# Seven-product FFN: shared sums finished in a PSUM bank, and the products of neighbouring pairs interleaved

## The chip, the cores and the metric

The kernel runs on one core of one Trainium2 chip. The metric is the device time of one execution in microseconds. Before the change, three runs gave 1776.2, 1776.36 and 1777.24 us; the median is 1776.36 us.

A core has TensorE (PE: matrix products, results into PSUM banks), VectorE (DVE), ScalarE (ACT), GpSimd (POOL), and DMA queues that are fed from SyncE (SP) and from GpSimd. Each engine works off its own list of instructions in order and waits on semaphores for the others. PEld in the profile is TensorE's weight load, which overlaps its products.

## The reference

Two layers of an encoder on 512 tokens of width 1024. Each layer has three token mixers (differential attention, a convolution module, neighbourhood attention), merged by gates and an output product, then an FFN and a gated per-layer input. The change is in the FFN:

```python
h = rmsnorm(x, norm_ffn[i])
x = x + (jax.nn.silu(h @ w_ffn_gate[i]) * (h @ w_ffn_up[i])) @ w_ffn_down[i]
```

The FFN is 2816 wide, that is 22 blocks of 128 columns. All is float32.

## The kernel before

Activations are held transposed: features on the 128 partitions, 512 tokens along the free dimension. A float32 product is done as three products of rounded halves: `split` (ScalarE copies the rounded part `hi`, line 143; VectorE subtracts for the rest `lo`, line 157), then hi x hi, hi x lo, lo x hi. So every block of weights is loaded by DMA, split by ScalarE and VectorE, and then used by TensorE.

In the FFN, gate and up product of one block of 128 columns are made together, in `seven` (a "pair"). The two weight blocks side by side and the tokens in two halves of 256 are taken as a 2 x 2 matrix product, which needs seven products of half size in place of eight (Winograd's form). The operands on the token side (b11, b21, b22 and the differences t1 to t4, called `bs`) are made once per layer in `quarters`, at the end of `w_o`. The operands on the weight side are a11, a12 (the gate's two halves), a22 (half of the up block) and the sums s1 to s4; s1 and s2 are summed by GpSimd's adding DMA (line 987) onto loads by SyncE (982, 983), s3 and s4 by VectorE (1003, 1007).

One `product` is four steps of 128 along the contraction, three matmuls of 256 columns each (lines 1017 to 1019): 12 matmuls. A pair has 84. The seven products of a pair run one after the other, in this order: a11b11, a22t4, s2t1, a12b21, s1t3, s3t2, s4b22. Three of them (p1 = a11b11, p4 = a22t4, p5 = s2t1) are needed alone and in a sum; ScalarE copies each to SBUF while its bank goes on collecting. Then VectorE combines: seven operations of 256 columns, which give gg (gate, times the norm's row factor `rb`) and uu (up). The first pair of a layer (`head`) has a different order and two more operations, because `rb` is not there yet. SiLU, the product with uu, and the split into `md` are put off (`pending`) and put out by `flush` in the next pair, behind its copy of p5.

The pairs take their three banks in turn from two groups: the three "mm" banks for an even block, the two "sc" banks and the "av" bank for an odd one. The two "tr" banks serve transposes, in the FFN those of the norm.

The 22 pairs of a layer fall into three parts of 8, 7 and 7 (`PARTS`). After each part the down projection adds its share to x: eight groups of products of 512 columns (`pair` and `gemm`, lines 177 to 179), each read by VectorE.

What sets the order: TensorE's instructions stand in program order. Those of the other engines are put in order by a planner at build time, which works through its own estimate of times and takes, on each engine, the ready instruction with the highest priority; priority is the place in the program, and what loads and splits weights is moved ahead by 400 instructions (`w_ahead`). A few orders are fixed by hand (`behind`). Split weights live in the rotating buffers `wh` and `wl`, three each; a pair uses two (a11|a12 and s1|s2), and the down projection uses the same. a22 has `kh` and `a`, s3|s4 have `spare`, one for even and one for odd blocks. A buffer's next split can begin when TensorE has used its last content. A counter (`chunk2`) gives a tick after every second product, and the norm's transposes and `rb` hang on ticks.

Of the kernel before, what the change touches and what calls it, by code (L numbers as in the profile page):

```python
# [14 lines left out]
AF = mybir.ActivationFunctionType  # L15
ALU = mybir.AluOpType
# [4 lines left out]
P = 128  # L21
# [40 lines left out]
class Net:  # L62
# [109 lines left out]
            self.low = self.split(hi[:, :n], lo[:, :n], raw[:, :n])  # L172
        return hi, lo

    def mm3(self, out, wh, wl, ah, al, first, last):
        mm = self.nc.tensor.matmul
        mm(out, wh, ah, start=first, stop=False)  # L177
        mm(out, wh, al, start=False, stop=False)  # L178
        mm(out, wl, ah, start=False, stop=last)  # L179

    def gemm(self, out, ap, acts, first=True, last=True):

# [661 lines left out]
    def diff_unit(self, head, qt, st4, k2, st, box, ys):  # L844

        nc, i = self.nc, self.i
        half, t = qt // 2, qt % 2
        box[qt] = self.probs(st4, k2, qt, box["s0"])
        if t == 0:
            return  # L850
        yield 3
        ats = [box[2 * half], box[2 * half + 1]]
        pps = []
        for kp in range(2):
            pt = self.ps("tr", (P, 2, 256))
# [12 lines left out]
        cs = slice((head % 2) * P, (head % 2) * P + P)  # L868
        for kp in range(2):
            for u in range(2):  # L870
                v = st["v", head // 2][kp][:, u].rearrange("p (a b) -> p a b", a=2)
                self.mm3(av[:, half * 256:half * 256 + 256], v[:, 0, cs], v[:, 1, cs],
                         pps[kp][:, 0, u], pps[kp][:, 1, u], kp * 2 + u == 0, kp * 2 + u == 3)
        if half == 0:
            return

        eps = self.sb("sm", [P, 4])
        self.stt(eps, box["s0"], EPS, box["s0"], ALU.mult, ALU.mult)
        o = self.sb("t", [P, 512])
# [61 lines left out]
    def quarters(self, x, h, j):  # L941


        one, two = slice(0, 256), slice(256, 512)
        g = lambda k: self.par(self.i, "ffn", k)
        f = []
        for k in (2 * j, 2 * j + 1):
            v = self.sb("t", [P, 512])
            self.act(v, x[k], AF.Copy, scale=g(k))
            f.append(v)  # L950
        b11, b12, b21, b22 = f[0][:, one], f[0][:, two], f[1][:, one], f[1][:, two]
        u = self.sb("t", [P, 2, 256])
        w = self.sb("t", [P, 2, 256])
        t1, t2, t3, t4 = u[:, 0], u[:, 1], w[:, 0], w[:, 1]
        self.tt(t1, b11, b12, ALU.subtract)
        self.tt(t2, b22, t1, ALU.add)
        self.tt(t3, b22, b12, ALU.subtract)
        self.tt(t4, t2, b21, ALU.subtract)
        if j < 2:
            d = [self.sb("rp", [P, 2, 256], F32R) for _ in range(2)]  # L960
            d += [self.sb("b", [P, 2, 256], F32R) for _ in range(2)] if j else \
                self.parts_of("v", [2, 256], 2, F32R)
        else:
            d = [q for n in range(2) for q in self.zs[2 * j - 4 + n]]
        for o, t in zip(d, (t1, t2, t3, t4)):
            self.held = self.split(o[:, 0], o[:, 1], t)
        ha, hb = self.halves(h[2 * j]), self.halves(h[2 * j + 1])
        cut = lambda p, c: (p[0][:, c], p[1][:, c])
        return dict(b11=cut(ha, one), b21=cut(hb, one), b22=cut(hb, two),
                    **{f"t{n + 1}": (o[:, 0], o[:, 1]) for n, o in enumerate(d)})  # L970

    def seven(self, wg, wu, bs, tags, spare, md, first, fb):


        nc = self.nc
        with self.tc.high_priority(offset=min(self.w_ahead, self.tc.cur_priority - self.p0)):
            lo, up = slice(0, 512), slice(512, 1024)
            g, a22 = self.sb("wr", [P, 1024]), self.sb("r", [P, 512])
# [24 lines left out]
            i = self.tt(s3, s1, a22, ALU.add)  # L1003
# [2 lines left out]
                self.behind(i, self.held if fb else self.mark)  # L1006
            self.tt(s4, s3, g[:, up], ALU.add)
            halve(*spare, sums[1], ("s3", "s4"))
        A, C, Q = (self.ps(t, (P, 2, 256)) for t in tags)

        def product(out, w, b, first):
            wh, wl = ws[w]
            mm = nc.tensor.matmul
            for k in range(4):
                c = slice(k * P, k * P + P)
                bh, bl = bs[k][b]
                mm(out, wh[:, c], bh, start=first and k == 0, stop=False, skip_group_check=True)  # L1017
                mm(out, wh[:, c], bl, start=False, stop=False, skip_group_check=True)  # L1018
                mm(out, wl[:, c], bh, start=False, stop=k == 3, skip_group_check=True)  # L1019
            self.chunk2()  # L1020

        o = self.sb("t", [P, 2, 256])
        p1, p4 = o[:, 0], o[:, 1]
        p5 = self.sb("a", [P, 256])
        gg, uu = self.sb("t", [P, 2, 256]), self.sb("t", [P, 2, 256])
        head = fb == 0
        product(A[:, 0], "a11", "b11", True)
        self.act(p1, A[:, 0], AF.Copy)
        if head:
            product(Q[:, 1], "a12", "b21", True)  # L1030
            product(C[:, 0], "s4", "b22", True)
        product(Q[:, 0], "a22", "t4", True)
        self.act(p4, Q[:, 0], AF.Copy)
        five = C[:, int(head)]
        product(five, "s2", "t1", True)
        self.flush(self.act(p5, five, AF.Copy))
        if not head:
            product(A[:, 0], "a12", "b21", False)
        product(Q[:, 0], "s1", "t3", False)
        product(A[:, 1], "s3", "t2", True)  # L1040
        if head:
            self.tt(gg[:, 0], Q[:, 1], p1, ALU.add)
            self.tt(gg[:, 1], C[:, 0], p5, ALU.add)
        else:
            product(C[:, 0], "s4", "b22", False)
        rb = self.rb.rearrange("p (a b) -> p a b", a=2)
        self.tt(p5, p4, p5, ALU.subtract)
        self.tt(gg[:, 0], gg[:, 0] if head else A[:, 0], rb[:, 0], ALU.mult)
        self.tt(p1, A[:, 1], p1, ALU.subtract)
        self.tt(uu[:, 0], p1, Q[:, 0], ALU.subtract)  # L1050
        self.tt(uu[:, 1], uu[:, 0], p5, ALU.add)
        self.tt(gg[:, 1], gg[:, 1] if head else C[:, 0], p1, ALU.subtract)
        self.tt(gg[:, 1], gg[:, 1], rb[:, 1], ALU.mult)

        def rest(then):
            i = self.act(gg, gg, AF.Silu, table="silu")
# [3 lines left out]
            self.held = self.split(*self.halves(md), gg.rearrange("p a b -> p (a b)"))  # L1060

        self.pending.append(rest)

    def behind(self, i, then):

# [17 lines left out]
    def ffn(self, h, x):  # L1083
# [6 lines left out]
        md8.append(tuple(self.sb("e", [P, 512], F32R) for _ in range(2)))  # L1090
        self.sums, self.sevens = [t for _ in range(2) for t in self.parts_of("qk", [1024], 2)], 0
        for part in PARTS:
            mids = []
            for f, fb in enumerate(part):
                tags = (("mm", "mm", "mm"), ("sc", "sc", "av"))[fb % 2]
                md = md8[f]
                mids.append(md)
                wg, wu = self.a["w_fg"][i, fb], self.a["w_fu"][i, fb]
                self.seven(wg, wu, bs, tags, spare[fb % 2], md, part[0] and f < 2, fb)
            self.flush()  # L1100
            down = [self.a["w_fd"][i, m][:, part[0] * P:(part[-1] + 1) * P] for m in range(KD)]
            two = [self.ps(("mm", "sc")[fb % 2 == 0]) for _ in range(2)]
            self.pair(two, down[:2], mids)
            for m in range(KD):
                if m < 2:
                    ps = two[m]
                else:
                    ps = self.ps("mm")
                    self.gemm(ps, down[m], mids)
                d = self.sb("t", [P, 512])  # L1110
                self.tt(d, ps, self.rb, ALU.mult)
                self.tt(x[m], x[m], d, ALU.add)
                if part is PARTS[-1]:
                    if m in (0, 2):
# [352 lines left out]
```

## Time and profile before

| What | Value |
|---|---|
| Median of three runs | 1776.36 us |
| The profiled execution, its span | 1776.7 us |
| TensorE busy | 1767.5 us (99%) |
| TensorE's weight loads busy | 1559.6 us (88%) |
| VectorE busy | 1421.7 us (80%) |
| ScalarE busy | 894.4 us (50%) |
| GpSimd busy | 103.0 us (6%) |
| Granted TensorE clock | digit 9 (90% or more) in every slice |

The profile is one execution, recorded by the hardware. An instruction's row has its start (us from the span's beginning), its duration, engine, line of the kernel, operation, and "out<-in" by the names of the tiles; a name begins with the stage that made it (`ffn_`, `wo_`, `pin_`). In brackets stands the idle time of the engine before it and what ended that. A group's row of waits has total, count and longest. Matmuls overlap in TensorE's pipeline, so the distance from start to start is what one costs, not its duration.

### The profile page before, as it was taken

How to read it: one execution, taken by the hardware profiler on the slowest of the kernel's cores; microseconds unless marked ns; L12 is line 12 of the kernel's file. 1: busy time of each engine (PE TensorE's matmuls, PEld its weight loads, DVE VectorE, ACT ScalarE, POOL GpSimd, SP SyncE). 2: the span in 40 equal slices, each digit the busy share in tenths (PEclk: the TensorE clock that was granted, in tenths of full speed). 3: DMA queues.
4: the chain of work that ended last, by engine and by line, in shares of the span. 5: the costliest groups of instructions: out<-in, count | busy, mean ns of one | idle time of the engine just before them, and what ended most of it. 6: DMA issues, size and time to landing. Idle time of an engine off the chain costs nothing.

```text
span 1776.7 us, 27451 instructions
## 1 busy us (share of the span) xinstructions
PE 1767.5 (99%) x10210; PEld 1559.6 (88%) x10210; DVE 1421.7 (80%) x2418; ACT 894.4 (50%) x1561; POOL 103.0 (6%) x146
## 2 busy tenths in 40 slices
PE   9999999999999999999999999999999999999998
PEld 7888888888899899998888888888888998989987
DVE  7878887998798587787776788889887976867776
ACT  5577555225565254454545765452356643534454
POOL 0000000000111010100000000000001110101000
PEclk9999999999999999999999999999999999999999
DMA  5666641334757366543447655423357664655332
GB/s 202 188 186 176 161 125 42 113 98 140 230 150 193 109 167 160 132 131 123 145 124 198 176 165 149 113 71 95 93 179 198 171 179 115 173 144 151 98 108 92
DMA packets 113509, 256.07 MB, mean 144 GB/s; under 512 B 14560, under 2 KB 19424, under 8 KB 113376
## 3 DMA queue, kind: packets, MB, share of 16 engines
q1 hardware_dynamic: 99984, 229.93, 42.3%
q0 software_dynamic: 12672, 23.07, 8.3%
q8 instruction: 81, 1.33, 0.3%
q10 hardware_dynamic: 720, 1.31, 0.2%
q14 instruction: 52, 0.43, 0.1%
HBM read 215.46 MB, written 7.34 MB: 125 GB/s over the span
## 4 chain that ended last, share of the span: by engine, by line
PE 96%; DVE 2%; ACT 1%; issue 0%; DMA 0%; POOL 0%; ACTq 0%; POOLq 0%; DVEq 0%
PE ffn_mm L1017 4%; PE ffn_mm L1019 4%; PE ffn_mm L177 4%; PE ffn_mm L179 4%; PE ffn_mm L178 4%; PE ffn_mm L1018 4%; PE ffn_sc L1019 3%; PE ffn_sc L1017 3%; PE ffn_sc L1018 3%; PE mergea_mm L177 2%; PE mergea_mm L178 2%; PE mergea_mm L179 2%; PE diff_sc L811 2%; PE gatec_mm L177 2%; PE gatec_mm L178 2%; PE gatec_mm L179 2%
## 5 line engine op out<-in xcount | busy, mean ns | idle before, releaser
L160 DVE SCALAR_TENSOR_TENSOR conv_z<-glu_z,pre_par,conv_z 128x512 f32<-128x512 f32 x240 | 179.4, 748 | 3.3
L143 ACT ACTIVATE ffn_wh<-ffn_wr 128x1024 fp32r<-128x1024 f32 (+1 forms) x92 | 92.7, 1014 | 111.7 <-PE ffn_mm L178 77.1
L987 POOL DMA_DIRECT2D ffn_qk<-w_fu x88 | 78.0, 990 | 605.7 <-DMA ffn_qk<-w_fu 414.7
L157 DVE TENSOR_TENSOR ffn_wl<-ffn_wr,ffn_wh 128x1024 fp32r<-128x1024 f32 (+1 forms) x92 | 107.4, 1173 | 5.4 <-ACT ffn_wh L143 4.9
L157 DVE TENSOR_TENSOR ffn_t<-ffn_mm,wo_rb 128x512 f32<-128x512 f32 (+1 forms) x64 | 38.6, 604 | 67.9 <-PE ffn_mm L179 67.8
L143 ACT ACTIVATE mergea_wh<-mergea_wr 128x1024 fp32r<-128x1024 f32 (+1 forms) x32 | 27.1, 846 | 96.8 <-PE mergea_mm L178 79.6
L143 ACT ACTIVATE ffn_wh<-ffn_qk 128x1024 fp32r<-128x1024 f32 x44 | 46.7, 1060 | 35.9 <-PE ffn_mm L178 15.7
L157 DVE TENSOR_TENSOR ffn_wl<-ffn_qk,ffn_wh 128x1024 fp32r<-128x1024 f32 x44 | 53.8, 1224 | 11.3 <-ACT ffn_wh L143 11.3
L157 DVE TENSOR_TENSOR ffn_t<-ffn_t,ffn_t 128x512 f32<-128x512 f32 (+1 forms) x46 | 31.3, 680 | 31.4 <-ACT ffn_t L143 30.9
L143 ACT ACTIVATE diff_a<-diff_sc,diff_s 128x512 f32<-128x512 f32 x32 | 22.0, 686 | 61.0 <-DVE diff_s L902 61.0
L177 PE MATMUL ffn_mm<-ffn_v,ffn_wh 128*128 128x512 f32 x132 | 51.4, 389 | 0.0
L178 PE MATMUL ffn_mm<-ffn_v,ffn_wh 128*128 128x512 f32 x132 | 51.4, 389 | 0.0
L179 PE MATMUL ffn_mm<-ffn_v,ffn_wl 128*128 128x512 f32 x132 | 51.3, 389 | 0.0
L177 PE MATMUL ffn_mm<-ffn_y,ffn_wh 128*128 128x512 f32 x132 | 51.3, 389 | 0.0
L178 PE MATMUL ffn_mm<-ffn_y,ffn_wh 128*128 128x512 f32 x132 | 51.3, 389 | 0.0
L179 PE MATMUL ffn_mm<-ffn_y,ffn_wl 128*128 128x512 f32 x132 | 51.3, 389 | 0.0
L1019 PE MATMUL ffn_mm<-wo_h,ffn_wl 128*128 128x256 f32 x176 | 49.8, 283 | 0.0
L1019 PE MATMUL ffn_sc<-wo_h,ffn_wl 128*128 128x256 f32 x176 | 49.8, 283 | 0.0
L1018 PE MATMUL ffn_mm<-wo_h,ffn_wh 128*128 128x256 f32 x176 | 49.8, 283 | 0.0
L1018 PE MATMUL ffn_sc<-wo_h,ffn_wh 128*128 128x256 f32 x176 | 49.8, 283 | 0.0
L1017 PE MATMUL ffn_sc<-wo_h,ffn_wh 128*128 128x256 f32 x176 | 49.8, 283 | 0.0
L1017 PE MATMUL ffn_mm<-wo_h,ffn_wh 128*128 128x256 f32 x176 | 49.8, 283 | 0.0
(876 smaller groups left out, 6588.6 us busy)
## 6 DMA issues: line engine op xcount, KB each, us to landing
ffn_qk<-w_fu POOLq DMA_DIRECT2D x88, 256.0 KB, 5.7
ffn_wr<-w_fg SPq DMA_DIRECT2D x44, 512.0 KB, 3.7
ffn_wr<-w_fd SPq DMA_DIRECT2D x32, 448.0 KB, 3.9
ffn_r<-w_fu SPq DMA_DIRECT2D x44, 256.0 KB, 3.7
ffn_qk<-w_fg SPq DMA_DIRECT2D x44, 256.0 KB, 4.3
ffn_qk<-w_fu SPq DMA_DIRECT2D x44, 256.0 KB, 4.6
natten_wr<-w_in SPq DMA_DIRECT2D x16, 512.0 KB, 4.3
natten_b<-bias SPq DMA_DIRECT2D x32, 256.0 KB, 4.0
```

What stands on the lines that cost most here:

```text
L143: i = self.nc.scalar.activation(out, in_, func, **kw)
L157: return self.nc.vector.tensor_tensor(out, a, b, op)
L160: return self.nc.vector.scalar_tensor_tensor(out, a, s, b, op0, op1)
L177: mm(out, wh, ah, start=first, stop=False)
L178: mm(out, wh, al, start=False, stop=False)
L179: mm(out, wl, ah, start=False, stop=last)
L811: self.nc.tensor.matmul(out, st4[:, u, qs], st[:, ks], start=n == 0, stop=n == 1)
L987: nc.gpsimd.dma_start(q, wu[:, lo], accum_op=ALU.add)
L1017: mm(out, wh[:, c], bh, start=first and k == 0, stop=False, skip_group_check=True)
L1018: mm(out, wh[:, c], bl, start=False, stop=False, skip_group_check=True)
L1019: mm(out, wl[:, c], bh, start=False, stop=k == 3, skip_group_check=True)
```

## The change

The seven products are the same. Three of the combinations now happen in the banks. The bank C gets a11b11; ScalarE copies it into the bank A; s3t2 is added onto it there (t2 and t4 have changed sign in `quarters`); ScalarE copies that sum from A into Q. Then A collects s2t1 and later s4b22, C collects a12b21, and Q collects a22t4. s1t3 goes to a bank of the "tr" group and is copied to `uu`; the sum in A after s2t1 is copied there too. VectorE is left with four operations: two sums for uu and the two products with `rb`. uu comes out with its sign turned, so the down projection's result is subtracted from x.

`seven` becomes a generator in steps, and `sevens_of` runs the steps of two neighbouring pairs in turn: step 1 of the next pair, step 4 of this one, step 2 of the next, step 5 of this one, step 3 of the next. For pairs after the first, this gives the order: next a11b11; this s2t1, a22t4; next s1t3; this s4b22; next s3t2, a12b21. The first pair of a part runs its steps 1 to 3 alone, the last its steps 4 and 5 alone. The first pair of a layer (`early`) has s4b22 in a "tr" bank, as its second product, followed by a12b21.

In the attention's `diff_unit` the two halves of the "av" bank now share one start flag (`mm3` passes on the extra argument).

```diff
-    def mm3(self, out, wh, wl, ah, al, first, last):
+    def mm3(self, out, wh, wl, ah, al, first, last, **kw):
...
-                         pps[kp][:, 0, u], pps[kp][:, 1, u], kp * 2 + u == 0, kp * 2 + u == 3)
+                         pps[kp][:, 0, u], pps[kp][:, 1, u], half + kp + u == 0,
+                         half * kp * u == 1, skip_group_check=True)
...
-        self.tt(t2, b22, t1, ALU.add)
+        self.stt(t2, t1, -1.0, b22, ALU.mult, ALU.subtract)
...
-        self.tt(t4, t2, b21, ALU.subtract)
+        self.stt(t4, t2, -1.0, b21, ALU.mult, ALU.subtract)
...
-        A, C, Q = (self.ps(t, (P, 2, 256)) for t in tags)
+        C, A, Q = (self.ps(t, (P, 256)) for t in tags)
...
+        def corner():
+            product(C, "a12", "b21")
+            if not early:
+                self.tt(gg[:, 0], C, self.halved(0), ALU.mult)
+
+        product(C, "a11", "b11", True)
+        self.act(A, C, AF.Copy)
+        yield
+        if early:
+            Z = self.ps("tr", (P, 256))
+            product(Z, "s4", "b22", True)
+            self.act(gg[:, 1], Z, AF.Copy)
+            corner()
+            yield
+        T = self.ps("tr", (P, 256))
+        product(T, "s1", "t3", True)
+        self.act(uu[:, 0], T, AF.Copy)
+        yield
+        product(A, "s3", "t2")
+        self.flush(self.act(Q, A, AF.Copy))
+        if not early:
+            corner()
+        yield
+        product(A, "s2", "t1")
+        self.act(uu[:, 1], A, AF.Copy)
+        product(Q, "a22", "t4")
+        self.tt(uu[:, 1], uu[:, 1], uu[:, 0], ALU.add)
+        self.tt(uu[:, 0], Q, uu[:, 0], ALU.add)
+        if early:
+            self.tt(gg[:, 0], C, self.halved(0), ALU.mult)
+            self.tt(gg[:, 1], A, gg[:, 1], ALU.add)
+        yield
+        if not early:
+            product(A, "s4", "b22")
+        self.tt(gg[:, 1], gg[:, 1] if early else A, self.halved(1), ALU.mult)
...
+    def sevens_of(self, pairs, head):
+        def go(*gens):
+            for g in gens:
+                next(g, None)
+        pairs = iter(pairs)
+        one = next(pairs)
+        go(one, one, one)
+        if head:
+            go(one)
+        for two in pairs:
+            go(two, one, two, one, two)
+            one = two
+        go(one, one)
...
-                self.tt(x[m], x[m], d, ALU.add)
+                self.tt(x[m], x[m], d, ALU.subtract)
```

The removed lines of `seven` are its block of products and the seven operations, which stand in the listing above.

More of the change, by code (lines that the diff above doesn't have):

```diff
@@ L173, in weights @@
         return hi, lo
-    def mm3(self, out, wh, wl, ah, al, first, last):
+    def mm3(self, out, wh, wl, ah, al, first, last, **kw):
         mm = self.nc.tensor.matmul
-        mm(out, wh, ah, start=first, stop=False)
-        mm(out, wh, al, start=False, stop=False)
-        mm(out, wl, ah, start=False, stop=last)
+        mm(out, wh, ah, start=first, stop=False, **kw)
+        mm(out, wh, al, start=False, stop=False, **kw)
+        mm(out, wl, ah, start=False, stop=last, **kw)
     def gemm(self, out, ap, acts, first=True, last=True):
@@ L970, in quarters, with seven @@
                     **{f"t{n + 1}": (o[:, 0], o[:, 1]) for n, o in enumerate(d)})
-    def seven(self, wg, wu, bs, tags, spare, md, first, fb):
+    def seven(self, wg, wu, bs, tags, spare, md, first, fb, early):
         nc = self.nc
@@ L1008, in seven, with product @@
             halve(*spare, sums[1], ("s3", "s4"))
-        A, C, Q = (self.ps(t, (P, 2, 256)) for t in tags)
-        def product(out, w, b, first):
+        C, A, Q = (self.ps(t, (P, 256)) for t in tags)
+        def product(out, w, b, first=False):
             wh, wl = ws[w]
@@ L1020, in product @@
             self.chunk2()
-        o = self.sb("t", [P, 2, 256])
-        p1, p4 = o[:, 0], o[:, 1]
-        p5 = self.sb("a", [P, 256])
         gg, uu = self.sb("t", [P, 2, 256]), self.sb("t", [P, 2, 256])
[L1026 to L1053, printed above, removed]
+        def corner():
+            product(C, "a12", "b21")
+            if not early:
+                self.tt(gg[:, 0], C, self.halved(0), ALU.mult)
@@ L1062, in seven, with halved @@
         self.pending.append(rest)
+    def halved(self, n):
+        return self.rb[:, n * 256:n * 256 + 256]
+    def sevens_of(self, pairs, head):
[11 more added lines that the diff above has]
+        go(one, one)
     def behind(self, i, then):
@@ L1092, in ffn @@
         for part in PARTS:
[L1093 to L1099, printed above, removed]
+            mids = md8[:len(part)]
+            self.sevens_of((self.seven(self.a["w_fg"][i, fb], self.a["w_fu"][i, fb], bs,
+                                       (("mm", "mm", "mm"), ("sc", "sc", "av"))[fb % 2],
+                                       spare[fb % 2], md8[f], part[0] and f < 2, fb, fb == 0)
+                            for f, fb in enumerate(part)), part[0] == 0)
             self.flush()
             down = [self.a["w_fd"][i, m][:, part[0] * P:(part[-1] + 1) * P] for m in range(KD)]
-            two = [self.ps(("mm", "sc")[fb % 2 == 0]) for _ in range(2)]
+            two = [self.ps(("mm", "sc")[part[-1] % 2 == 0]) for _ in range(2)]
             self.pair(two, down[:2], mids)
```

## The prediction

> **What bounds the kernel now.** I read the page's shares and chain first, then TensorE's waits, then the windows of the stage that is changed, then three stretches of its timelines.
>
> ```profile
> span 1776.7 us, 27451 instructions
> ...
> PE 1767.5 (99%) x10210; PEld 1559.6 (88%) x10210; DVE 1421.7 (80%) x2418; ACT 894.4 (50%) x1561; POOL 103.0 (6%) x146
> ...
> PE 96%; DVE 2%; ACT 1%; issue 0%; DMA 0%; POOL 0%; ACTq 0%; POOLq 0%; DVEq 0%
> ```
>
> TensorE is busy for 99% of the span and is 96% of the chain that ended last. Its own waits in the whole program are four:
>
> ```profile
> PE pre_av L325 <- DVE pre_zeror L398: 1.1, 1, 1.1
> PE natten_tr L734 <- ACT natten_e L143: 0.3, 2, 0.2
> PE natten_tr L736 <- ACT natten_e L143: 0.3, 2, 0.2
> PE natten_tr L736 <- DVE natten_a L157: 0.2, 1, 0.2
> ```
>
> None is in the FFN, which is what the change touches. Busy spans of overlapping matmuls can hide small holes, so I count starts too. The window from the first product of layer 0 to the end of the eighth pair:
>
> ```profile
> 495.93:577.09 81.16, 81.16 (x681) 81.16 (x680) 72.92 (x125) 48.95 (x81) 13.51 (x15) 1.00 0.70 179
> ```
>
> The columns are PE, PEld, DVE, ACT, POOL, clock, DMA. Eight pairs are 8 x 7 x 12 = 672 matmuls plus 8 transposes; at one start each 0.12 us the matmuls alone are 80.6 of the 81.16 us. The 0.12 us and the length of a product come from these rows (the first rows of the layer's products):
>
> ```profile
> 495.93 0.28 PE L1017 MATMUL ffn_mm<-wo_h,ffn_wh 128*128 128x256 f32 x1
> ...
> 497.24 0.28 PE L1019 MATMUL ffn_mm<-wo_h,ffn_wl 128*128 128x256 f32 x1
> 497.36 0.28 PE L1017 MATMUL ffn_mm<-wo_h,ffn_wh 128*128 128x256 f32 x1
> ...
> 498.80 0.60 PE L213 MATMUL wo_tr<-pre_ident,wo_ss 128*128 128x128 f32 x4
> 499.15 0.36 PE L1017 MATMUL ffn_mm<-wo_h,ffn_pt 128*128 128x256 f32 x1
> ```
>
> A product takes 497.36 - 495.93 = 1.43 us, a pair 7 x 1.43 = 10.0 us. So the FFN runs at TensorE's issue rate without a hole. What the other engines save there is worth nothing by itself; the change can gain only by a faster matmul, and can lose by any wait it puts before one.
>
> **The change, part by part.** *TensorE.* 84 matmuls of the same width per pair before and after, with the same weights and moving operands in each of the seven products; the down projection is untouched. Cost 0. The tick that issues the norm's two groups of transposes still falls after the second and the sixth product: cost 0.
>
> *VectorE.* The block behind the products shrinks from seven operations of 256 columns to four (gg0, two sums for uu, gg1):
>
> ```profile
> 641.93 0.42 DVE L157 TENSOR_TENSOR ffn_a<-ffn_t,ffn_a 128x256 f32<-128x256 f32 x1
> ...
> 644.05 0.42 DVE L157 TENSOR_TENSOR ffn_t<-ffn_t,wo_rb 128x256 f32<-128x256 f32 x1
> ```
>
> These are the first and the last of the seven. 42 pairs save 3 each, the two first pairs 9 - 5 = 4 each: 134 x 0.42 = 56 us of VectorE's 1421.7. TensorE covers all of it now, so it is worth 0. Subtracting in place of adding into x costs the same. Eight of `quarters`' 32 additions per layer become the three-operand form; One of them on 256 columns can hardly cost more than twice the 0.42, so 0 to 16 x 0.42 = 7 us of VectorE, near 0 by the nearest row, and covered likewise (the last quarter's operands are wanted no earlier than the fourth product, as now).
>
> *ScalarE.* Three copies out of the banks become four (C to A, T to uu, A to Q, A to uu), five in a first pair: 42 + 4 = 46 more. No row shows a copy that writes a bank; the rows below give 0.36 to 0.38 for one that reads it, and wo_z's row further down 0.40 from SBUF to SBUF, so about 0.36 to 0.40, some 17 us in all on an engine that is 50% busy. What counts is when they end, since TensorE now waits for three of them. The steady pair, ScalarE:
>
> ```profile
> 642.35 0.38 ACT L143 ACTIVATE ffn_t<-ffn_mm 128x256 f32<-128x256 f32 x1 [2.05 <-PE ffn_mm L1019]
> 643.66 0.63 ACT L143 ACTIVATE ffn_kh<-ffn_r 128x512 fp32r<-128x512 f32 x1 [0.92 <-PE ffn_mm L1018]
> 644.20 0.36 ACT L143 ACTIVATE ffn_t<-ffn_mm 128x256 f32<-128x256 f32 x1
> 645.21 0.38 ACT L143 ACTIVATE ffn_a<-ffn_mm 128x256 f32<-128x256 f32 x1 [0.65 <-PE ffn_mm L1019]
> 645.49 0.62 ACT L143 ACTIVATE ffn_t<-ffn_t 128x512 f32<-128x512 f32 x1
> 646.58 1.06 ACT L143 ACTIVATE ffn_wh<-ffn_qk 128x1024 fp32r<-128x1024 f32 x1 [0.47 <-ACT ffn_t L143]
> 647.55 0.61 ACT L143 ACTIVATE ffn_v<-ffn_t 128x512 fp32r<-128x512 f32 x1
> 648.07 1.04 ACT L143 ACTIVATE ffn_y<-ffn_qk 128x1024 fp32r<-128x1024 f32 x1
> 649.01 1.04 ACT L143 ACTIVATE ffn_wh<-ffn_wr 128x1024 fp32r<-128x1024 f32 x1
> ```
>
> It idles for 2.05, 0.92 and 0.65 us in front of work that TensorE releases. The new steady order, with "one" the earlier pair and "two" the next, is: two a11b11, one s2t1, one a22t4, two s1t3, one s4b22, two s3t2, two a12b21. Copy A to Q must end before one's s2t1, with two products between (2.87 us); A to uu before s4b22, two products (2.87 us); C to A before s3t2, four products (5.7 us). Today's copies have two, two and three products to spare. A copy of 0.38 behind one split of 1.06 is 1.44 us, half of the room. Cost 0.
>
> *Buffers for weights.* The split pieces (`wh`, `wl`: three buffers, two used per pair) are freed in another order. The piece s1|s2 of the next pair takes the buffer of a11|a12; the row at 646.58 shows it start just when a12's product has ended:
>
> ```profile
> 646.45 0.28 PE L1017 MATMUL ffn_mm<-wo_v,ffn_wh 128*128 128x256 f32 x1
> ...
> 647.68 1.23 DVE L157 TENSOR_TENSOR ffn_wl<-ffn_qk,ffn_wh 128x1024 fp32r<-128x1024 f32 x1 [0.23 <-ACT ffn_wh L143]
> ```
>
> The first row starts the product after a12's. Both halves are done at 648.91, 2.5 us after the release. Now five products (7.2 us) lie between release and use; after the change three (4.3 us): 1.8 us to spare, each pair. For a11|a12 the room goes from nine products to five, for s3|s4 from twelve to seven. Cost 0, but this is the thinnest place of the steady state. The loads themselves (SP's four and POOL's two adding ones per pair) are the same; they are issued three products earlier in the program and still wait for the same raw buffers; the adding load's 5.7 us to landing is far below a 10 us pair with three raw buffers.
>
> ```profile
> ffn_qk<-w_fu POOLq DMA_DIRECT2D x88, 256.0 KB, 5.7
> ```
>
> *The first pair of a layer.* Its order becomes a11b11, s4b22, a12b21, s1t3, s3t2. The third product adds into C, so it waits until C is copied to A, and only one product lies between. ScalarE at this place now:
>
> ```profile
> 497.79 0.40 ACT L143 ACTIVATE wo_z<-wo_t 128x256 fp32r<-128x256 f32 x1
> 498.10 0.58 ACT L143 ACTIVATE pin_t<-pin_sc 128x512 f32<-128x512 f32 x1
> 498.57 0.40 ACT L143 ACTIVATE wo_z<-wo_t 128x256 fp32r<-128x256 f32 x1
> 498.88 1.06 ACT L143 ACTIVATE ffn_wh<-ffn_qk 128x1024 fp32r<-128x1024 f32 x1
> 499.85 0.70 ACT L143 ACTIVATE wo_z<-wo_t 128x256 fp32r<-128x256 f32 x2
> 500.46 0.58 ACT L143 ACTIVATE pin_t<-pin_sc 128x512 f32<-128x512 f32 x1
> 500.94 0.37 ACT L143 ACTIVATE ffn_t<-ffn_mm 128x256 f32<-128x256 f32 x1
> ```
>
> The last row is the copy of the same a11b11 product, which ended at about 497.5: it came 3.4 us late, behind work that is earlier in the program, and nobody minded. The third product is due at 499.15. If the copy stood where it stands now, TensorE would wait until 501.31 + 0.1 (a hand-over as above): 2.2 us. But the 1.06 us split at 498.88 needs the buffer that a12b21 frees (it starts right at that release), so it falls behind the copy: the two wo_z go to 498.88, pin_t to 499.5, the copy to about 500.0, the third product to about 500.45. Wait 1.3 us. If the planner takes the copy in the slot at 498.10, the wait is 0. I take 1.3, by the row it is nearest to, per layer; both ends, 0 and 2.2, stay for the range. Behind this wait stand all later products; what feeds them has then 1.3 us more room.
>
> *The ends of the three parts.* The last pair of a part has no partner, so its A to Q copy has one product of room (1.43 us) and its A to uu copy likewise, with the next down-projection splits in the queue. ScalarE does at such an end now:
>
> ```profile
> 572.92 1.06 ACT L143 ACTIVATE ffn_wh<-ffn_wr 128x1024 fp32r<-128x1024 f32 x1 [0.47 <-ACT ffn_t L143]
> 573.89 0.61 ACT L143 ACTIVATE ffn_y<-ffn_t 128x512 fp32r<-128x512 f32 x1
> 574.41 1.04 ACT L143 ACTIVATE ffn_wh<-ffn_wr 128x1024 fp32r<-128x1024 f32 x1
> ```
>
> The first copy meets an idle engine: 0. For the second, count from the end of a12b21: split 1.0, md half to 1.6, second split (released at 1.4, ahead in priority) to 2.6, copy to 2.95, against 2.87 due: 0.15 us of wait with the hand-over, or 0 if copy and split change places, or 0.35 if the md half ends 0.2 later. I take 0.07 x 6 = 0.4, between the first two. First pairs of parts 2 and 3 need C to A within one product, with one 1.06 us split released 1.43 us before: 0.
>
> Sum: 2 x 1.3 + 0.4 + zeros = +3.0 us. The profiled execution was 1776.7 us, 0.3 above the median of 1776.36; on the median this is 1779.4.
>
> **A page of the Trainium skill against the row.** Three rows of TensorE's timeline, two neighbours in the first pair and the start of a product in a steady one:
>
> ```profile
> 501.62 0.28 PE L1019 MATMUL ffn_mm<-wo_z,ffn_a 128*128 128x256 f32 x1
> 501.73 0.28 PE L1017 MATMUL ffn_mm<-wo_z,ffn_kh 128*128 128x256 f32 x1
> ...
> 642.15 0.28 PE L1017 MATMUL ffn_mm<-wo_v,ffn_kh 128*128 128x256 f32 x1
> ```
>
> The first two are 0.11 us apart, where a product's mean is 1.43 / 12 = 0.12. The Trainium skill ("TensorE: Matmul & The Clock Gate", Back-to-back issue gap) gives N / 2.4 + 2.5 ns, 109 ns for 256 columns, as the warm gap of an isolated stream; by it a pair is 0.9 us shorter than the trace has it, and something would be holding TensorE. The trace does not agree, and the measurement decides.
>
> **The rivals.**
> (1) *Hidden anyway.* ScalarE's planner puts the copy into an early slot, all other room holds: +0, 1776.4. For it: the gaps above; against it: the copy that came 3.4 us late.
> (2) *Slower, by the steady state.* The split of s1|s2 slips past its 1.8 us. It now stands behind the A to Q copy and the SiLU, and the SiLU waits for gg1, whose product ended only one product before. It decides when ScalarE reaches the split more than 1.8 us after the release. 38 pairs have a predecessor in their part; at 0.3 us each +11 us, 1791 with the first pairs; at 0.7, 1806. Against it: copy and SiLU are 0.38 + 0.62 = 1.0 us and start one product, 1.43 us, before the release; VectorE is lighter than now.
> (3) *More at the first pair.* The copy at its present place (2.2 us a layer), A to Q late as well and the ends at their worst (6 x 0.35): 4.4 + 2.1 = 6.5, 1782.9.
> (4) *Faster matmuls.* The 0.12 us is held up by VectorE's or ScalarE's traffic and falls to the 0.11 that some rows have: 44 x 84 x 0.01 = 37 us, 1739. Against it: from 642.15 to the row at 646.45 three products take 1.43 us each while ScalarE idles for a third of the time, the same as at 495.93, where it has no gap.
>
> **How the numbers follow.** The forecast (wait of one to two microseconds in each layer's first pair, little else; 1778.4 to 1781) gets 0.45, hidden 0.22, steady state 0.18, more at the first pair 0.10, faster matmuls 0.05. About what a measurement can tell from no change is 0.2%, 3.55 us, so the line lies at 1779.9. Of the forecast two thirds are under it. Faster: 0.05. Same: 0.30 + 0.22 = 0.52. Slower: 0.15 + 0.18 + 0.10 = 0.43. The range takes in the forecast, hidden, more at the first pair, and the lower third of the steady state: 1775.6 to 1788, leaving out some 0.17; the forecast's own is 1778.4 to 1781.
>
> **What the changed profile would show.** A wait of TensorE at the third product of each layer, for ScalarE's copy, 1 to 1.5 us long, with the copy right behind a pin_t; no other TensorE wait in the FFN over 0.3 us; the window of eight pairs 81 to 83 us long; VectorE's busy time some 56 us lower, ScalarE's 17 higher; 0.12 us between the products' matmuls. The prediction is wrong if waits recur in each pair at s1t3, s2t1 or s4b22, or if the copy is taken at once.

## The result and the profile after

The changed kernel takes 1782.47 us (median of five runs, 1781.2 to 1784.88), the kernel before 1776.36 (1776.2 to 1777.24): the ratio is 1.0034, with a 95% interval from 1.0022 to 1.0045. The change costs some 6 us, about twice the forecast's 3; that is a third of a per cent, small but clear of the noise.

The page of the changed kernel, its span, busy times and chain:

```profile
span 1783.1 us, 27425 instructions
...
PE 1773.3 (99%) x10210; PEld 1561.7 (88%) x10210; DVE 1377.8 (77%) x2284; ACT 917.0 (51%) x1607; POOL 103.4 (6%) x146
...
PE 95%; DVE 3%; ACT 1%; issue 1%; POOL 0%; DMA 0%; ACTq 0%; POOLq 0%; DVEq 0%
```

VectorE has 44 us less to do and ScalarE 23 us more. TensorE does the same 10210 matmuls, is still 99% busy, and gets longer. Its own waits (total, count, longest):

```profile
PE ffn_mm L1020 <- DVE ffn_pt L157: 2.0, 2, 1.0
PE pre_av L325 <- DVE pre_zeror L398: 1.1, 1, 1.1
PE wo_tr L227 <- POOL wo_rc L223: 0.4, 2, 0.2
```

The first and the last are new. Both come once in each layer, and neither is the one that was forecast. The window from the first product of layer 0 to the end of its eighth pair:

```profile
498.73:582.43 83.70, 82.47 (x682) 81.51 (x681) 66.16 (x103) 53.38 (x90) 13.76 (x15) 0.95 0.70 176
```

It was 81.16 us and is 83.70 (the window ends 0.1 us into the down projection). How long a layer's FFN takes on TensorE is read from its first product to the last transposes that bear its name, those of the norm behind it. These rows give the transposes' first and last start, of the kernel before:

```profile
L227 PE MATMUL ffn_tr<-pre_ident,ffn_rc x4: 271/272/273, 848.8 to 849.1; 128*128 128x128 f32 x4
```

and the same group and the first product, of the changed kernel:

```profile
L227 PE MATMUL ffn_tr<-pre_ident,ffn_rc x4: 271/272/278, 854.2 to 854.5; 128*128 128x128 f32 x4
...
498.73 0.28 PE L1018 MATMUL ffn_mm<-wo_h,ffn_wh 128*128 128x256 f32 x1
```

Before: 849.1 - 495.93 = 353.2 us. After: 854.5 - 498.73 = 355.8 us. With hundredths from the starts it is 353.17 and 355.77 in both layers: 2.60 us more per layer, 5.2 in all. That is the change. (This one execution began the first layer's FFN 2.7 us later than the same kernel did when it was profiled once more: 498.73 against 496.04. The span of the second profile is 2.6 us shorter, so these 2.6 us don't belong to the change; the last section comes back to it.)

Where the 2.60 us of a layer lie is seen by comparing each matmul's start with the next one's, 0.12 us apart where nothing waits:

| Place in the layer | Longer than before, us |
|---|---|
| third pair, s3t2 | 0.21 + 0.10 + 1.16 + 0.10 = 1.57 |
| second pair, the norm's last transposes | 0.33 |
| first pair, s1t3 | 0.14 + 0.10 = 0.24 |
| end of part 1, s4b22 | 0.11 + 0.10 = 0.21 |
| ends of parts 2 and 3, s4b22 | 0.08 + 0.08 = 0.16 |
| sum | 2.5 of 2.6 |

The largest is the third pair's s3t2. TensorE there, in the changed kernel:

```profile
523.03 0.28 PE L1020 MATMUL ffn_sc<-wo_h,ffn_y 128*128 128x256 f32 x1
523.36 0.39 PE L1018 MATMUL ffn_mm<-wo_rp,ffn_pt 128*128 128x256 f32 x1
523.59 0.28 PE L1019 MATMUL ffn_mm<-wo_rp,ffn_pt 128*128 128x256 f32 x1
524.87 0.39 PE L1020 MATMUL ffn_mm<-wo_rp,ffn_pt 128*128 128x256 f32 x1 [1.00 <-DVE ffn_pt L157]
```

`ffn_pt` is the buffer of s3|s4 of this pair. VectorE in the same stretch:

```profile
519.19 0.69 DVE L157 TENSOR_TENSOR ffn_v<-ffn_t,ffn_v 128x512 fp32r<-128x512 f32 x1
519.79 0.68 DVE L157 TENSOR_TENSOR ffn_qk<-ffn_qk,ffn_r 128x512 f32<-128x512 f32 x1
520.39 1.22 DVE L157 TENSOR_TENSOR ffn_wl<-ffn_wr,ffn_wh 128x1024 fp32r<-128x1024 f32 x1
521.53 0.68 DVE L157 TENSOR_TENSOR ffn_qk<-ffn_qk,ffn_wr 128x512 f32<-128x512 f32 x1
...
523.60 1.22 DVE L157 TENSOR_TENSOR ffn_pt<-ffn_qk,ffn_pt 128x1024 fp32r<-128x1024 f32 x1
```

The first row is the end of the split of the first pair's result into `md`. The second is the sum s3 of the third pair, right behind it; the fourth is s4; the last is the low half of s3|s4, done at 524.82, where TensorE wanted it with its third matmul at 523.7. The same work in the kernel before:

```profile
516.90 0.68 DVE L157 TENSOR_TENSOR ffn_v<-ffn_t,ffn_v 128x512 fp32r<-128x512 f32 x1
517.50 0.68 DVE L157 TENSOR_TENSOR ffn_qk<-ffn_qk,ffn_r 128x512 f32<-128x512 f32 x1
...
520.25 1.23 DVE L157 TENSOR_TENSOR ffn_pt<-ffn_qk,ffn_pt 128x1024 fp32r<-128x1024 f32 x1
```

Counted from the layer's first product, VectorE begins its half of `md`'s split at 20.97 us before and 20.46 after, and the low half of s3|s4 is done at 25.55 and 26.09: nearly the same. What moved is the use. s3t2 was the twentieth product and is the seventeenth; it starts 28.09 us after the first product before (at 524.02) and 24.63 after. The 2.8 us of room turned into a wait of 1.2. That s3 comes directly behind `md` is no accident of VectorE: `seven` sets an order for s3 by hand in the first three pairs of a layer (`if first or fb < 3: self.behind(i, self.held ...)`), and in the third pair what it stands behind is the split of the first pair's `md`.

The step that the forecast had priced, a12b21 in the first pair, shows no wait. ScalarE at this place:

```profile
500.59 0.36 ACT L143 ACTIVATE ffn_mm<-ffn_mm 128x256 f32<-128x256 f32 x1
500.89 1.42 ACT L143 ACTIVATE wo_z<-wo_t 128x256 fp32r<-128x256 f32 x4
502.22 1.07 ACT L143 ACTIVATE pin_t<-pin_sc 128x512 f32<-128x512 f32 x2
503.17 0.39 ACT L143 ACTIVATE ffn_t<-ffn_tr 128x256 f32<-128x256 f32 x1
```

The first row is the copy from C to A. It is done at 500.95, a microsecond ahead of a12b21 (501.97); the `wo_z` and `pin_t` copies come behind it, not ahead. What is late instead is the last row, the copy of s4b22 out of the "tr" bank: s1t3, due at 503.48, needs that bank and starts at 503.61. And the norm's small sums, VectorE first, then GpSimd:

```profile
502.78 0.69 DVE L216 TENSOR_REDUCE wo_sm<-wo_tr 128x4 f32<-128x512 f32 x1
...
503.72 1.22 DVE L157 TENSOR_TENSOR ffn_wl<-ffn_wr,ffn_wh 128x1024 fp32r<-128x1024 f32 x1
504.85 1.22 DVE L157 TENSOR_TENSOR ffn_wl<-ffn_qk,ffn_wh 128x1024 fp32r<-128x1024 f32 x1
...
506.59 0.17 DVE L219 TENSOR_SCALAR wo_sm<-wo_sm 128x4 f32<-128x4 f32 x1
```

```profile
506.84 1.46 POOL L223 TENSOR_TENSOR wo_rc<-wo_sm,pre_power 128x4 f32<-128x4 f32 x1 [8.89 <-DVE wo_sm L219]
```

Two weight splits got between the reduction and the small sum behind it, so GpSimd ends at 508.30, and the transposes that were due at 508.0 start at 508.35.

### The profile page after: what moved, and what is told of

Read it like the earlier page. It is cut to its first block, busy times and chain, and to the rows that moved or that the text cites. A ratio compares the mean times of both kernels' runs of the same rounds, so it can differ in the third digit from the quotient of the medians.

```text
span 1783.1 us, 27425 instructions
## 1 busy us (share of the span) xinstructions
PE 1773.3 (99%) x10210; PEld 1561.7 (88%) x10210; DVE 1377.8 (77%) x2284; ACT 917.0 (51%) x1607; POOL 103.4 (6%) x146
## 4 chain that ended last, share of the span: by engine, by line
PE 95%; DVE 3%; ACT 1%; issue 1%; POOL 0%; DMA 0%; ACTq 0%; POOLq 0%; DVEq 0%
PE ffn_mm L178 4%; PE ffn_mm L177 4%; PE ffn_mm L179 4%; PE ffn_mm L1020 3%; PE ffn_mm L1018 3%; PE ffn_mm L1019 3%; PE ffn_sc L1018 3%; PE ffn_sc L1020 3%; PE ffn_sc L1019 3%; PE mergea_mm L178 2%; PE mergea_mm L177 2%; PE mergea_mm L179 2%; PE diff_sc L811 2%; PE gatec_mm L177 2%; PE gatec_mm L178 2%; PE gatec_mm L179 2%
## 5 line engine op out<-in xcount | busy, mean ns | idle before, releaser
L157 DVE TENSOR_TENSOR ffn_t<-ffn_mm,wo_rb 128x512 f32<-128x512 f32 (+1 forms) x86 | 47.8, 556 | 71.7 <-PE ffn_mm L179 61.4
L143 ACT ACTIVATE natten_wh<-natten_wr 128x1024 fp32r<-128x1024 f32 x24 | 25.4, 1058 | 41.7 <-issue 15.2
```

Source lines behind the costliest of these rows:

```text
L143: i = self.nc.scalar.activation(out, in_, func, **kw)
L157: return self.nc.vector.tensor_tensor(out, a, b, op)
```

## The experiments

All ratios are against the kernel before on the same chip, whose medians were 1776.8 to 1777.13 us on the three chips used; the column "Against before" is the one to compare. "FFN" is the stretch measured above, one layer.

| Kernel | Median, us | Ratio, 95% interval | Against before, us | FFN, us |
|---|---|---|---|---|
| before | | | | 353.17 |
| the change again | 1782.29 | 1.0032, 1.0019 to 1.0044 | +5.2 | 355.76 |
| shorter hold | 1779.24 | 1.0013, 1.0004 to 1.0022 | +2.1 | 354.25 |
| + norm's sums earlier | 1778.51 | 1.0008, 1.0000 to 1.0017 | +1.4 | 353.86 |
| no interleaving | 1794.29 | 1.0098, 1.0085 to 1.0112 | +17.2 | 361.57 |
| + bank and part ends | 1776.88 | 1.0002, 0.9992 to 1.0011 | +0.1 | 353.23 |
| VectorE's work given back | 1778.82 | 1.0012, 1.0004 to 1.0021 | +2.0 | 354.15 |
| before, hold and flag alone | 1777.02 | 1.0001, 0.9992 to 1.0010 | +0.2 | 353.17 |
| the copy late | 1783.95 | 1.0037, 1.0023 to 1.0051 | +6.9 | 356.76 |

**The change again.** The changed kernel as it is, beside the experiments.

> The changed kernel as it is, on the same chip as its variants. Its profile lost time in two ways: 1.7 us in the opening, where this one execution was granted a clock of 0.949 for the first 36 us, and 5.1 us in the FFN (2.55 per layer). If the opening belongs to that execution alone, this profile has the opening as before and TensorE's waits in the FFN as before: 1.16 us for ffn_pt at the third pair of each layer, 0.34 at wo_tr, 0.24 at the first pair's s1t3. Then the median is 5 to 6 us over the kernel before. If the opening's loss belongs to the change, it is there again.

It measured 1782.29 us (1781.23 to 1783.68), with the same new waits of TensorE, 1.0 us for `ffn_pt` in each layer. The opening is as before: the first FFN product starts at 496.04 us, against 495.93 in the kernel before. So the opening's loss belonged to the one execution. (The expectation has the lower clock in its first 36 us alone; the trace has 0.95 in the FFN's window too.)

**The hold one pair shorter.** The hand-set order no longer covers the third pair.

```diff
-            if first or fb < 3:
+            if first or fb < 2:
                 self.behind(i, self.held if fb else self.mark)
```

> The changed kernel, but the order by hand that puts the third pair's s3 = s1 + a22 behind the split of the first pair's result is dropped (fb < 2 in place of fb < 3). Theory: in the new order that result is split later and s3|s4 is needed earlier, so this order by hand makes TensorE wait 1.16 us (1.6 with the matmuls beside it) at the third pair's s3t2; without it the wait goes, 3 us in two layers. Rival: s3|s4 is late because VectorE's queue is full there (a split of 1.22 us stands between s3 and s4); then dropping the order moves it by less than 0.5 us.

1779.24 us, 3.0 us less than the change. TensorE's waits start like this, with none in the FFN's products:

```profile
PE pre_av L325 <- DVE pre_zeror L398: 1.1, 1, 1.1
PE wo_tr L227 <- POOL wo_rc L223: 0.4, 2, 0.2
```

VectorE makes the third pair's sums and the low half before the first pair's `md`:

```profile
509.94 0.69 DVE L157 TENSOR_TENSOR ffn_qk<-ffn_qk,ffn_r 128x512 f32<-128x512 f32 x1
...
512.69 1.23 DVE L157 TENSOR_TENSOR ffn_pt<-ffn_qk,ffn_pt 128x1024 fp32r<-128x1024 f32 x1
...
517.00 0.69 DVE L157 TENSOR_TENSOR ffn_v<-ffn_t,ffn_v 128x512 fp32r<-128x512 f32 x1
```

s3t2 starts at 519.97 here, 6 us after the low half is done. So the hold was the cause, and VectorE had the time. It accounts for 1.5 of the 2.6 us a layer.

**The norm's small sums earlier as well.** Their priority is raised above that of the weight splits, and so is that of the copy of s4b22 in a layer's first pair.

```diff
-        with self.tc.high_priority(offset=min(200, ...) ...):
+        with self.tc.high_priority(offset=min(600 if self.phase == "wo" else 200, ...) ...):
             sm = self.sb("sm", [P, 4])
...
-            self.act(gg[:, 1], Z, AF.Copy)
+            with self.tc.high_priority(offset=min(400, self.tc.cur_priority - self.p0)):
+                self.act(gg[:, 1], Z, AF.Copy)
```

> The changed kernel without that order, and with two instructions moved ahead in priority: the norm's small sums in front of the first pair's splits (TensorE waited 0.34 us at wo_tr), and the copy of Z ahead of the copies of the input product (TensorE waited 0.24 us for its bank). Theory: the three waits are all that the FFN lost except the end of a part, so the FFN comes within 0.5 us of its time before and the run within 1 us (0.06%) of the kernel before. Rival: something of the change that is not a wait in the FFN costs the rest; then 2 us or more stay.

1778.51 us. The transposes' wait is gone, and the FFN is 0.39 us a layer shorter. It is still 0.7 us a layer above the kernel before and the run 1.4, where the theory had the run within 1 us. The copy did not move, and s1t3's delay (0.15 + 0.10 us) stayed. Priority alone didn't bring that copy forward, and the part ends were not touched here.

**No interleaving.** The changed kernel, with all five steps of one pair ahead of the next pair's.

```diff
-        for two in pairs:
-            go(two, one, two, one, two)
-            one = two
-        go(one, one)
+        for one in pairs:
+            go(one, one, one, one, one, one)
```

(The three lines ahead of the loop, which start the first pair, go too.)

> The changed kernel without the interleaving: each pair runs its seven products in one piece. Theory: then each copy between banks has one product (1.43 us) of room in every pair, as it now has at the ends of parts, where 0.08 to 0.22 us were lost; three such places in 44 pairs give 0.1 to 0.3 us a place, 13 to 40 us slower than the change. Rival: a copy takes 0.4 us and needs no more than 1.43; then it costs under 3 us and the interleaving was worth nothing.

1794.29 us, 12.0 us more than the change, just under the 13 to 40 expected. TensorE's waits in the FFN:

```profile
PE ffn_sc L1018 <- ACT ffn_t L143: 2.6, 2, 1.3
PE ffn_mm L1018 <- ACT ffn_t L143: 1.9, 2, 1.0
...
PE ffn_mm L1018 <- ACT ffn_mm L143: 0.9, 2, 0.5
PE ffn_mm L1020 <- DVE ffn_pt L157: 0.9, 2, 0.4
```

These lie in the first three pairs of a layer. Most of the later pairs add about 0.21 us in front of s4b22, too short for the list of waits: the copy from A to `uu` has one product of room in each pair here, which in the change only the last pair of a part has. So the interleaving pays for itself: the copies through the banks need the second product between them.

**The remaining short rooms.** On top of the shorter hold and the earlier norm: the first pair's bank for s4b22 comes from the "av" group, and in the last pair of a part s1t3 moves behind a22t4.

```diff
-            Z = self.ps("tr", (P, 256))
+            Z = self.ps("av", (P, 256))
...
-        T = self.ps("tr", (P, 256))
-        product(T, "s1", "t3", True)
-        self.act(uu[:, 0], T, AF.Copy)
-        yield
+        def side():
+            T = self.ps("tr", (P, 256))
+            product(T, "s1", "t3", True)
+            self.act(uu[:, 0], T, AF.Copy)
+        if not tail:
+            side()
+            yield
...
         product(Q, "a22", "t4")
+        if tail:
+            side()
```

(The raised priority of the copy of s4b22 is taken back; in the last pair, the flush of the pair before it goes one step further down.)

> The version with the shorter hold, the norm's earlier small sums, and two more edits: the first pair's bank for s4b22 comes from the av group (so s1t3 no longer waits for its copy), and in the last pair of a part s1t3 stands behind a22t4, so that two products lie between each ScalarE copy and its use. Theory (what is left of the loss are these single short rooms): the waits in front of s1t3 (0.25 us a layer) and at the end of part 1 (0.2 us a layer, 0.08 at parts 2 and 3) go, 1 to 1.3 us in all; the FFN's TensorE starts take 683.0 to 683.3 us where the kernel before takes 682.9, and the run is within 0.5 us of the kernel before. Rival (something steady costs TensorE a little in each pair): it stays 1 us or more above the kernel before. Second rival (the moved product only shifts the wait, to the down projection's first splits behind md): no gain over the version before it, 1.4 us above the kernel before.

1776.88 us against 1776.8 for the kernel before. The FFN takes 353.23 us a layer against 353.17; the FFN's matmul starts alone, which the expectation counts over both layers with the work between them left out, add up to 683.0 us against 682.9. The only wait at the head of TensorE's list is an old one outside the FFN:

```profile
PE pre_av L325 <- DVE pre_zeror L398: 1.1, 1, 1.1
```

So the places in the table of the result explain the loss, and nothing steady is left in the pairs. The new order, mended, is as fast as the old one; no version here is faster.

**VectorE's work given back.** The version with the norm's earlier sums, with three additions per pair whose result nothing uses.

```diff
         self.tt(uu[:, 0], Q, uu[:, 0], ALU.add)
+        dump = self.sb("t", [P, 2, 256])
+        for _ in range(3):
+            self.tt(dump[:, 0], uu[:, 0], uu[:, 1], ALU.add)
```

> The version with the shorter hold and the norm's earlier small sums, plus three VectorE additions of 256 columns in each pair, whose results nothing uses: VectorE gets back about what the change took from it (132 x 0.33 to 0.42 = 44 to 55 us). Theory (VectorE's saved time is covered by TensorE and worth nothing): the same time as that version within 0.5 us, 1.4 us above the kernel before, and VectorE's busy time back at 1420 us. Rival (the lighter VectorE is what keeps the new order's waits small): 3 us or more slower than that version, with waits of TensorE for VectorE's subtractions in the FFN.

```profile
PE 1768.6 (100%) x10210; PEld 1559.2 (88%) x10210; DVE 1419.4 (80%) x2416; ACT 910.3 (51%) x1607; POOL 108.0 (6%) x146
```

VectorE is back at 1419.4 us, 42 more than without the additions. The run is 1778.82 us, 2.0 above the kernel before where the version without them is 1.4 above, and the FFN is 0.29 us a layer longer: 0.28 of it in front of the second pair's s4b22. The intervals of the two runs overlap; the rows of the two layers give 0.58 us. So 42 us of VectorE are worth about 0.6 us. That is a little over the 0.5 that I had allowed, and far from the rival's 3.

**Two parts on the old order.** The kernel before, with the shorter hold and the attention's shared start flag.

```diff
-                         pps[kp][:, 0, u], pps[kp][:, 1, u], kp * 2 + u == 0, kp * 2 + u == 3)
+                         pps[kp][:, 0, u], pps[kp][:, 1, u], half + kp + u == 0,
+                         half * kp * u == 1, skip_group_check=True)
...
-            if first or fb < 3:
+            if first or fb < 2:
```

> The kernel before, with two things alone: the shared start flag of the attention's av bank, and the shorter hand-set order (pairs 1 and 2 of a layer in place of 1 to 3). Theory (the hold costs only together with the new order, and the flag costs nothing): 0 within 0.5 us, and no wait of TensorE in the FFN. Rival (the hold is a loss in either order, so that the shorter one is a gain of its own): 2 to 3 us faster than the kernel before, which would make the mended version's gain no property of the change.

1777.02 us against 1776.8, and the same 353.17 us a layer. The hold costs nothing in the old order, and neither does the flag.

**The copy late.** The changed kernel, with the order that the forecast had assumed: in a layer's first pair, the copy from C to A stands behind the token operands' last split.

```diff
-        self.act(A, C, AF.Copy)
+        i = self.act(A, C, AF.Copy); early and self.behind(i, self.held)
```

> The changed kernel, with one order by hand: in a layer's first pair the copy of a11b11 from bank C into bank A stands behind the last split of the token-side operands (the t4 of quarters), so that ScalarE has it behind the wo_z and pin_t copies, which is where the forecast put it. Theory (the forecast's wait is real where the copy is late, and it did not come because ScalarE took the copy at once): TensorE waits 1.5 to 2.2 us in front of a12b21 in each layer, for the copy; the third pair's wait for the subtraction stays at 1.0 us, since both of its ends move along with TensorE; the run is 3 to 4.5 us slower than the changed kernel, 1785 to 1787 us. Rival (the later work catches up: a wait early in the layer gives the splits behind it room, and later waits shrink by as much): less than 1.5 us slower than the changed kernel, with the third pair's wait gone or halved.

1783.95 us. Against the kernel before that is 6.9, where the change has 5.2: 1.7 us more, between the two expectations. (The two were measured on different chips and their intervals overlap; the FFN's rows, 356.76 against 355.76, are what the reading rests on.) ScalarE, with the copy in the last row:

```profile
498.23 1.02 ACT L143 ACTIVATE wo_z<-wo_t 128x256 fp32r<-128x256 f32 x3
499.14 0.58 ACT L143 ACTIVATE pin_t<-pin_sc 128x512 f32<-128x512 f32 x1
499.62 0.38 ACT L143 ACTIVATE ffn_t<-ffn_tr 128x256 f32<-128x256 f32 x1
499.89 0.39 ACT L143 ACTIVATE ffn_mm<-ffn_mm 128x256 f32<-128x256 f32 x1
```

TensorE's row at a12b21, and the head of its list of waits:

```profile
500.33 0.38 PE L1018 MATMUL ffn_mm<-wo_h,ffn_wh 128*128 128x256 f32 x1 [1.40 <-ACT ffn_mm L143]
...
PE ffn_mm L1018 <- ACT ffn_mm L143: 2.8, 2, 1.4
PE ffn_mm L1020 <- DVE ffn_pt L157: 2.0, 2, 1.0
```

The wait is real, and by starts it costs 1.58 us a layer more than the change has there. The third pair's wait stays at 1.0, as the theory had it: both of its ends move with TensorE. But the FFN grows by 1.00 us only, since the two small waits behind it are gone: s1t3's 0.25 (its bank is copied out meanwhile) and the norm's 0.33 (its small sums have the time). I had counted those two in the theory's price as if they stayed.

## Why the prediction was right or wrong

The sum was +3.0 us on the median. The FFN shows +5.2. The measured time, 1782.47, lies inside the range but above the forecast's own 1778.4 to 1781, and the forecast's mechanism did not happen: the wait that was priced measured 0, and most of the loss, 2.14 of 2.6 us a layer, came from places that the sum had at 0 or not at all. That the direction and the range hold is in good part luck.

- *What bounds the kernel.* Right. TensorE's issue rate is the limit, and a wait put in front of it is paid, less what later waits shrink by: the late copy's 1.58 us lengthened the FFN by 1.00. 42 us of VectorE's work moved the time by 0.6.
- *TensorE at cost 0.* Right. Three products of a steady pair take 643.26 - 638.95 = 4.31 us in the rows further down, 1.44 each as before, and no matmul waits there. The rival of faster matmuls (1739) falls.
- *VectorE, -56 us.* The count, 134 instructions fewer, is right; the size is 44. Added up over the traces, the durations fell by 54.6 us (1552.4 to 1497.8), but 44 / 134 is 0.33 us each. Neighbours overlap, so an instruction's duration of 0.42 is more than it adds; its distance to the next start is what counts, as the last two rows below show. The three-operand form takes 0.42 us, like the addition, which is the low end that I took.
- *ScalarE, +17 us.* The 46 copies are right; the size is 23. The copies that write a bank take 0.36 to 0.37 us, inside the bounds. Most of the other 6 us is lost overlap: added up over the traces, ScalarE's durations grew by 18.0 us (983.2 to 1001.2, in the change again), and the time in which neighbours overlap fell from 88.9 to 84.1 us.
- *Steady rooms, cost 0.* Right, with the thinnest place where it was put. TensorE's rows are the starts of the product after a12b21 and of s1t3, of the changed kernel when it was profiled again:

```profile
638.95 0.28 PE L1018 MATMUL ffn_mm<-wo_h,ffn_wh 128*128 128x256 f32 x1
...
643.26 0.28 PE L1018 MATMUL ffn_tr<-wo_v,ffn_wh 128*128 128x256 f32 x1
```

ScalarE's and VectorE's split of s1|s2, and two neighbouring sums on VectorE:

```profile
639.08 1.06 ACT L143 ACTIVATE ffn_wh<-ffn_qk 128x1024 fp32r<-128x1024 f32 x1 [0.47 <-ACT ffn_t L143]
```

```profile
640.17 1.23 DVE L157 TENSOR_TENSOR ffn_wl<-ffn_qk,ffn_wh 128x1024 fp32r<-128x1024 f32 x1 [0.45 <-ACT ffn_wh L143]
...
646.34 0.42 DVE L157 TENSOR_TENSOR ffn_t<-ffn_av,ffn_t 128x256 f32<-128x256 f32 x1
646.67 0.41 DVE L157 TENSOR_TENSOR ffn_t<-ffn_sc,wo_rb 128x256 f32<-128x256 f32 x1
```

The split starts at the release and ends at 641.40, 1.86 us ahead of its use, where 1.8 was forecast. The second rival (1791) falls: SiLU and copy are done before the release.

- *The first pair, 1.3 us a layer.* This step failed: it measured 0, its lower end. ScalarE took the copy at once. The price itself held: with the copy forced behind `pin_t`, TensorE waits 1.40 us. What failed is "by the row it is nearest to": the copy's late place in the old program said nothing of its place in the new one. Why the planner now takes it first isn't settled. In the changed kernel VectorE splits a22 ahead of this quarter's sums, so the first `wo_z` copy becomes ready only as ScalarE comes free; no run has tested whether that decides it.
- *"for s3|s4 from twelve to seven. Cost 0"*. This is the step that the loss hides in: 1.57 us a layer. I counted the room from the release of the buffer. At the third pair of a layer the release isn't what lets s3 start; the hand-set order behind the first pair's `md` is, as the shorter hold shows. Seven products of room on paper were less than none at the third pair.
- *The part ends, 0.07 each.* The place is right; the size is 0.21 at part 1 and 0.08 at the others, 0.37 a layer in place of 0.21.
- *The norm's tick at cost 0.* It does fall after the same products, but what hangs on it came late: 0.33 us a layer. *s4b22's "tr" bank* had no term at all: 0.24 us a layer.

Of the rivals, the first (hidden) had the copy right and the rest of the room wrong. The third's 1782.9 is nearest to the measured time, but its mechanism, a copy still later, didn't come either.

Of the signs listed ahead, VectorE's direction, the unchanged 0.12 us and the absence of recurring waits came. The wait at the third product didn't; two others in the FFN are over 0.3 us (1.57 and 0.33 by the starts); and the window of eight pairs is 83.7 us, over the 81 to 83. The copy was taken at once, which the prediction itself had named as a sign that it is wrong.

## What to carry to other kernels

When an operand's use moves forward, ask what its producer really waits for: a buffer's release, or an order someone set by hand for the old sequence. Go through every such order in the code, and compare its end with the new use, in the first rounds of a loop above all, where the room is smallest. While one engine never idles, work saved on the others is worth next to nothing (here 0.6 us for 42), and a place in another engine's queue must be computed for the new program, not read off the old one.

## What the runs showed of the hardware

*A restart costs about 0.1 us.* Where a product's matmul had to wait, the one after it also starts about 0.10 us late: 523.59 comes 0.23 us after 523.36, where two neighbours are 0.12 apart, and 0.39 us is the first one's duration in place of 0.28. The wait listed at 1.00 us costs 1.26 by the starts, the one listed at 1.40 (the copy late) 1.66. At the end of part 1 a start that is 0.11 us late costs 0.21, and the list of waits doesn't show it at all: short waits are found by comparing starts.

*The FFN didn't feel a clock 5% lower.* The profiled execution of the changed kernel and its second profile, span and mean granted clock:

```profile
core 0: 1783.1 us, clock 0.948
```

```profile
core 0: 1780.5 us, clock 0.999
```

At 0.95 (the window above has it in the FFN too) a layer's FFN took 355.77 us, at 1.00 it took 355.76. The 2.6 us between the spans all lie ahead of the first FFN product; whether the clock is their cause is not shown. The Trainium skill ("TensorE: Matmul & The Clock Gate", Back-to-back issue gap) has the spacing of isolated matmuls follow the clock: N / 1.2 ns when cold, N / 2.4 + 2.5 ns when warm. If the pace here followed the clock in that way, the FFN would have been some 5% longer, an estimate by that rule. This trace does not agree. Between 0.95 and 1.00, at 0.12 us a matmul of 256 columns, something other than the granted clock sets the pace; what it is, no run here shows, and two profiles say nothing of lower clocks.
